# A hybrid diffusion block in fp32 on one Trainium2 core: the weights of one modulation step as one tile and one DMA of 2048 columns

## The chip, the cores and the metric

The kernel runs on one core of a Trainium2 chip. The metric is the device time of one execution in microseconds. Before the change it is 1861.96 us, the median of 3 runs (1861.82 to 1862.53).

## The reference

A backbone block over 512 latent tokens and 256 context tokens of width 1024, with two layers in fp32. Layer 0 mixes with a Hyena long convolution beside a spatial gating unit, layer 1 with a recurrent block (RG-LRU); each layer then has a SwiGLU of inner width 2816. What the change touches is the modulation: each layer scales, shifts and gates by vectors that come from the condition c (latents) and c_ctx (context).

```python
silu_c = jax.nn.silu(c)
silu_cc = jax.nn.silu(c_ctx)
for l in range(DEPTH):
    mod_x = (silu_c @ w_ada[l] + b_ada[l]).reshape(-1, 1, N_MOD, D_MODEL)
    hx = modulate(rmsnorm(x, norm_mix_g[l]), mod_x[:, :, 0], mod_x[:, :, 1])
    ...
        mod_c = (silu_cc @ w_ada[l] + b_ada[l]).reshape(1, 1, N_MOD, D_MODEL)
    ...
    x = x + mod_x[:, :, 2] * mix_x
    hx = modulate(rmsnorm(x, norm_ffn_g[l]), mod_x[:, :, 3], mod_x[:, :, 4])
    x = x + mod_x[:, :, 5] * swiglu(hx, w_ffn_in[l], w_ffn_out[l])
```

w_ada is 2 x 1024 x 6144 in fp32, 50 MB in all: a product of two vectors with a large matrix, which is read once.

## The kernel before, in words

All activations stand with channels on the 128 partitions and tokens along the row. A large product is split in high and low fp32r halves and made of three matmuls (hi by hi, hi by lo, lo by hi). Weights come by DMA from SP's queue into one of three `raw` tiles (`load_w`, L230), are split by `halve` (L247 casts to `whi`, L248 subtracts to `wlo`) on ACT, DVE or POOL, and then stand ready for the PE. SP's queue is in order: a DMA that waits for its tile to come free holds up all that stand behind it.

The modulation is the class `Ada` (L317 to L355). `Ada(l, r)` makes 2048 of the 6144 columns for layer l (r = 0, 1, 2). It has 8 steps, one for each 128 rows of w_ada. In a step k, `load` (L323 to L330) brings 128 x 2048 weights in pieces of `ada["w"]` columns, one tile and one DMA each, from a ring of `ada["b"]` tiles of the pool; `mm` (L332 to L338) makes four matmuls (L336), one for each 512 columns. Each has the 128 x 32 tile `sct` as its stationary operand (columns 0 and 1 hold silu of c and c_ctx for this k, the rest is zero) and writes 32 partitions of one PSUM tile, quarter q to partitions 32q to 32q+31. After step 7 the sums are copied (L341), transposed (L344) and become `mod[l][r]`.

Six of them are made, beside other work: `Ada(0, 0)` and `Ada(0, 1)` in the first 190 us with 3 tiles of 1024 columns, `Ada(0, 2)` in the latent long convolutions (`fwd_x`, `inv_x`, 330 to 392 us) with 4 tiles of 512 columns, and `Ada(1, 0)` to `Ada(1, 2)` in layer 0's SwiGLU (495 to 940 us) with 3 tiles of 512 columns, so that the fourth piece of a step waits for the first piece's matmul. In the SwiGLU `post` calls the steps, one or more after each pair of hidden tiles (the list `fill`). The order on each engine is not the order of the source: the framework's scheduler places every instruction by a simulated timeline when the program is built, and it may put the four matmuls of a step apart with other matmuls between them.

Small constants (gains, biases, convolution taps, c) come as one tile `prm` of 289 columns by one DMA (L212, L213); `pc(name)` returns a slice of it.

Of the kernel before, what the change touches and what calls it, by code (L numbers as in the profile page):

```python
# [8 lines left out]
F32 = mybir.dt.float32  # L9
F32R = mybir.dt.float32r  # L10
I32 = mybir.dt.int32
AF = mybir.ActivationFunctionType
# [4 lines left out]
P = 128  # L17
D = 1024
KD = D // P
# [9 lines left out]
EPS = 1e-6  # L29
# [18 lines left out]
PCOLS = {}  # L48
_n = 0
for _name, _w in (("b_ada0", 48), ("b_ada1", 48), ("mix_g0", 8), ("mix_g1", 8), ("ffn_g0", 8), ("ffn_g1", 8),  # L50
                  ("fin_g", 8), ("hcw", 36), ("hcb", 12), ("skip", 8), ("ln_g", 4), ("rcw", 44), ("rcb", 11),
                  ("lam", 22), ("c", 16)):
    PCOLS[_name] = (_n, _w)
    _n += _w
NPC = _n

PARTS = [[(i, min(i + 4, NPAIR)) for i in range(0, NPAIR, 4)], [(0, 20), (20, 22)]]

# [118 lines left out]
def program(tc, A, out):  # L177
    nc = tc.nc
    act, dve, pool, pe = nc.scalar, nc.vector, nc.gpsimd, nc.tensor
    f = lambda t: t.bitcast(F32)  # L180
# [3 lines left out]
    def op(name, side="left", **kw):  # L184
        cm = tc.tile_pool(name=name, bufs=1, side=side, **kw)
        opened.append(cm)
        return cm, cm.__enter__()

    def cl(cm):
        opened.remove(cm)  # L190
        cm.__exit__(None, None, None)

    _, cst = op("cst")
# [7 lines left out]
    def nm(s):  # L201
        cnt[0] += 1
        return f"{s}_{cnt[0]}"
# [4 lines left out]
    def smt():  # L208
        return ps.tile([P, 512], F32, tag="sm", bufs=4, name=nm("sm"))


    prm = cst.tile([P, NPC], F32, name="prm")  # L212
    nc.sync.dma_start(prm, A["prm"])  # L213

    def pc(name):
        o, w = PCOLS[name]
        return prm[:, o:o + w]

    ident = cst.tile([P, P], F32, name="ident")
    make_identity(nc, ident)  # L220
# [52 lines left out]
    class Job:  # L273
# [6 lines left out]
        def mm(self, b, k):  # L280
            wh, wl = self.w
            xh, xl = self.x(b, k)
            n = self.n[b]
            self.n[b] += 1
            for pi, (w, x) in enumerate(((wh, xh), (wh, xl), (wl, xh))):
                pe.matmul(self.outs[b], w[:, k * P:(k + 1) * P], x,  # L286
                          start=(n == 0 and pi == 0), stop=(n == self.nk - 1 and pi == 2))
# [4 lines left out]
    def newton(pl, src, n, scale, eps, tag):  # L292
        v = pl.tile([P, n], F32, tag=tag + "v", name=nm("nv"))
        y = pl.tile([P, n], F32, tag=tag + "y", name=nm("ny"))
        t = pl.tile([P, n], F32, tag=tag + "t", name=nm("nt"))
        dve.tensor_scalar(v, src, scale, eps, op0=ALU.mult, op1=ALU.add)
        yi = y.bitcast(I32)
        dve.tensor_single_scalar(yi, v.bitcast(I32), 1, op=ALU.logical_shift_right)
        dve.tensor_scalar(yi, yi, -1, 0x5F3759DF, op0=ALU.mult, op1=ALU.add)
        dve.tensor_scalar_mul(v, v, -0.5)  # L300
        for _ in range(3):
            dve.tensor_mul(t, y, v)
            dve.tensor_mul(t, t, y)
            dve.scalar_tensor_tensor(y, t, 1.5, y, op0=ALU.add, op1=ALU.mult)
        return y


    sct = cst.tile([P, KD, 32], F32, name="sct")
    dve.memset(sct, 0.0)
    mod = [[None] * 3, [None] * 3]  # L310
    ada = {"b": 3, "w": 1024}

    class Ada:
# [17 lines left out]
        def mm(self, k):  # L331
            l, r = self.l, self.r  # L332
            if k == 0:
                self.ps = smt()
            for q in range(4):
                pe.matmul(self.ps[32 * q:32 * q + 32, :], sct[:, k, :],  # L336
                          self.w[k, q],
                          start=(k == 0), stop=(k == KD - 1))  # L338
            if k == KD - 1:
                sb = ada["p"].tile([P, 512], F32, tag="ada", bufs=ada["b"], name=nm("adas"))  # L340
                act.copy(sb, self.ps)  # L341
                pt = smt()
                for q in range(4):
                    pe.transpose(pt[:, P * q:P * (q + 1)], sb[:, P * q:P * (q + 1)], ident)  # L344
                m = cst.tile([P, 2, 16], F32, name=f"mod{l}{r}")
                for v in range(2):
                    dve.tensor_add(m[:, v, :].rearrange("p (j q) -> p j q", q=4),
                                   pt.rearrange("p (q j s) -> p j q s", q=4, j=4)[:, :, :, v],
                                   pc(f"b_ada{l}")[:, 16 * r:16 * r + 16].rearrange("p (j q) -> p j q", q=4))
                mod[l][r] = m  # L350
# [9 lines left out]
    def ab(l, which):  # L360
        g = pc(f"mix_g{l}" if which == "mix" else f"ffn_g{l}")
        sc = mod[l][0][:, :, 8:16] if which == "mix" else mod[l][2][:, :, 0:8]
        sh = mod[l][0][:, :, 0:8] if which == "mix" else mod[l][1][:, :, 8:16]
        a = cst.tile([P, 2, 8], F32, name=f"A{l}{which}")
        for v in range(2):
            dve.scalar_tensor_tensor(a[:, v, :], sc[:, v, :], 1.0, g, op0=ALU.add, op1=ALU.mult)
        return a, sh
# [84 lines left out]
    HALF = [(0, 384), (384, 768)]  # L452


    cm_h, hp = op("h")
    cm_ada, ada["p"] = op("ada")
    cm_zb, zb = op("zb", "right")
# [30 lines left out]
    ktl = [kf.tile([P, 1024], F32R, name=f"ktl{i}") for i in range(2)]  # L488
    kdram = {}
    nfil = {}  # L490
    nfs = cst.tile([P, 16], F32, name="nfs")
    for s in "xc":
        for order in range(2):
            nfil[s, order] = 4 * len(nfil)
# [163 lines left out]
    s01.load()  # L658
    ada0.load(1)
    pool.memset(hd2[64:65, :], 1.0)  # L660
    act.activation(sct[:, :, 0], pc("c")[:, 0:8], AF.Silu)
    act.activation(sct[:, :, 1], pc("c")[:, 8:16], AF.Silu)
    s00.prep()
    s10.load_f3w()
    load_x(1)
# [91 lines left out]
    hcw, hcb = pc("hcw"), pc("hcb")  # L757
# [70 lines left out]
    for i, c in enumerate((19, 12, 13, 14, 15)):  # L828
# [6 lines left out]
        for _ in range(2):  # L835
            if len(fill) > 0:
                fill.pop(0)()
    nfy = newton(cst, nfs, 16, 0.5, EPS, "nf")
    cl(cm_nt)
    cl(cm_kf)  # L840
    cm_za, za = op("za", "right")
# [28 lines left out]
    skip = pc("skip")  # L870
# [136 lines left out]
    cl(cm_h)  # L1007
    cm_hy, hy = op("hy")
    ada["p"] = hy
    ada["b"] = 4  # L1010
    ada["w"] = 512
    for i in range(2, 4):
        load_dt(hy, i, dtr[i - 2])
    ada2.load(0)
# [29 lines left out]
    cl(cm_hy)  # L1044
    cl(cm_eo)
    cl(cm_dt)


    _, c2 = op("c2")
    _, xp = op("x")  # L1050
    cm_xc, xc = op("xc")
    cm_ada, ada["p"] = op("adaB")
    ada.update(b=3, w=512)
    cm_nt, ntp = op("ntB")
    cm_g, gp = op("g0")
    xt = []
# [433 lines left out]


    lam = pc("lam")
    sp = [c2.tile([P, 22], F32, name=f"sp{i}") for i in range(5)]
    cq = c2.tile([P, 22], F32, name="cq")
    cq2 = c2.tile([P, 22], F32, name="cq2")
    hba = c2.tile([RDH, 64], F32, name="hba")
# [10 lines left out]
    for cf in (1.0 / 120.0, 1.0 / 24.0, 1.0 / 6.0, 0.5, 1.0, 1.0):  # L1507
        dve.tensor_mul(ee, ee, rr)
        dve.tensor_scalar(ee, ee, cf, None, op0=ALU.add)
    ni = c2.tile([P, 22], I32, name="ni")  # L1510
    dve.tensor_scalar(nn, nn, 127.0, 8388608.0, op0=ALU.add, op1=ALU.mult)
    dve.tensor_copy(ni, nn)
    dve.tensor_mul(ee, ee, ni.bitcast(F32))
# [11 lines left out]
    dve.tensor_scalar_mul(cq, ee, 2.0)  # L1525
    dve.tensor_scalar_mul(cq2, ee, -4.0)
    dve.tensor_scalar_mul(hba, hba, 0.5)
    fill = Ada(1, 0).steps() + Ada(1, 1).steps() + Ada(1, 2).steps()
    cm_hf, hf = op("hf0")

# [15 lines left out]
    rcw, rcb = pc("rcw"), pc("rcb")  # L1546
# [184 lines left out]
    for j in range(NR):  # L1731
        a, b = rg_chunk(j)
# [30 lines left out]
    for b, (t0, t1) in enumerate(BLK1):  # L1763
# [7 lines left out]
        for k in range(KD):  # L1771
            o = hf.tile([P, 256], F32, tag=f"b{k}{'hl'[b]}", name=nm("o"))
# [27 lines left out]
```

## Time and profile before

| | |
|---|---|
| median of 3 runs | 1861.96 us |
| profiled execution: its time | 1861.27 us |
| profiled execution: span from first to last instruction | 1859.5 us |
| mean granted TensorE clock | 0.962 |
| busy: PE, DVE, ACT, POOL | 93%, 68%, 39%, 33% of the span |
| matmuls of the modulation (L336) | 121.1 us of PE busy time, 384 records of 192 matmuls |

A matmul of fp32 operands leaves two records in this profile, so 384 records are 192 matmuls (6 x 8 x 4). The profiled execution's own time is 0.7 us below the median. In a timeline row, columns are start, duration, engine, line, operation, out<-in, shape, count, and in brackets the idle time before it with what ended it. Ends of matmuls are modelled, so what a matmul costs is read from the start before it to the start after it.

### The profile page before, as it was taken

To read this page: it belongs to the slowest core of one execution; us is meant where nothing else is said; L and a number is where in the kernel's file an instruction comes from. 1 tells how busy PE (TensorE), PEld (TensorE's weight loads), DVE (VectorE), ACT (ScalarE), POOL (GpSimd) and SP (SyncE) were. 2 spreads that over 40 slices of the span, in tenths; PEclk is the share of its full clock that TensorE was granted. 3 is DMA by queue.
4 is the path that set the end of the run, shared out by engine and by line. 5 is a ranking of instruction groups with operands and counts; after the bars stand their busy time and mean duration, and the time that the engine had idled before them with its cause. 6 is when DMAs were issued, how large, how long until landed. Compare 5 with 4: busy or idle time off the path is not lost. (4 is left out here: it accounts for less than half of the span.)

```text
span 1859.5 us, 23986 instructions
## 1 busy us (share of the span) xinstructions
PE 1728.6 (93%) x8968; PEld 1433.9 (77%) x8968; DVE 1265.4 (68%) x1963; ACT 726.2 (39%) x1144; POOL 616.6 (33%) x518
## 2 busy tenths in 40 slices
PE   5999999899999999999999988888997799999996
PEld 2576888579868978998798867667786678888886
DVE  7865766566887866887688785879889733333225
ACT  3543333222434333433343435666655332222212
POOL 4332132442465554564545421444444200000002
PEclk8999999899999999999999989889998899999998
DMA  8746232724243343213522124444453132222321
GB/s 285 238 139 229 86 122 81 242 89 142 64 125 112 99 143 123 67 63 119 159 68 69 63 65 129 119 114 116 125 134 93 66 114 91 94 99 80 91 80 46
DMA packets 92077, 213.02 MB, mean 115 GB/s; under 512 B 9001, under 2 KB 34745, under 8 KB 91961
## 3 DMA queue, kind: packets, MB, share of 16 engines
q1 hardware_dynamic: 89593, 204.68, 35.3%
q0 software_dynamic: 1792, 6.29, 0.9%
q8 instruction: 70, 1.15, 0.3%
q10 hardware_dynamic: 576, 0.52, 0.1%
q14 instruction: 46, 0.38, 0.1%
HBM read 178.30 MB, written 11.53 MB: 102 GB/s over the span
## 5 line engine op out<-in xcount | busy, mean ns | idle before, releaser
L248 DVE TENSOR_TENSOR wlo<-raw,whi 128x512 fp32r<-128x512 f32 (+2 forms) x300 | 308.2, 1042 | 275.9 <-ACT whi L247 270.5
L247 ACT CAST whi<-raw 128x1024 fp32r<-128x1024 f32 (+2 forms) x228 | 193.7, 858 | 415.4 <-PE mm L263 178.5
L386 POOL TENSOR_TENSOR ssum<-ssum,sq 128x256 f32<-128x256 f32 (+2 forms) x37 | 37.7, 1022 | 443.7 <-ACT sq L384 423.2
L336 PE MATMUL sm<-ada,sct 128*32 128x512 f32 x384 | 121.1, 635 | 3.9 <-issue 3.0
L1104 PE MATMUL sm<-yh,whi 128*128 128x256 f32 (+1 forms) x304 | 96.4, 323 | 21.8 <-DVE x L1067 11.1
L248 POOL TENSOR_TENSOR wlo<-raw,whi 128x1024 fp32r<-128x1024 f32 (+1 forms) x31 | 76.4, 2464 | 111.8 <-DVE whi L247 38.8
L286 PE MATMUL sm<-hh,whi 128*128 128x512 f32 (+1 forms) x248 | 93.5, 378 | 7.2 <-ACT whi L247 4.0
L1104 PE MATMUL sm<-yh,wlo 128*128 128x256 f32 (+1 forms) x304 | 95.9, 317 | 1.8 <-POOL wlo L248 1.8
L286 PE MATMUL sm<-hh,wlo 128*128 128x256 f32 (+1 forms) x248 | 92.4, 378 | 5.0 <-DVE wlo L248 2.9
L1104 PE MATMUL sm<-yl,whi 128*128 128x256 f32 (+1 forms) x304 | 95.9, 316 | 0.0
L286 PE MATMUL sm<-hl,whi 128*128 128x512 f32 (+1 forms) x248 | 92.3, 372 | 0.0
L247 DVE CAST whi<-raw 128x512 fp32r<-128x512 f32 (+2 forms) x103 | 67.9, 660 | 33.8 <-PE sm L1279 26.1
L1104 PEld LDWEIGHTS sm<-yh,whi 128*128 128x128 f32 x304 | 60.8, 202 | 25.8 <-DVE x L1067 12.2
L263 PE MATMUL mm<-hl,whi 128*128 128x512 f32 (+1 forms) x256 | 69.2, 344 | 0.0
L263 PE MATMUL mm<-hh,wlo 128*128 128x512 f32 (+1 forms) x256 | 68.9, 346 | 0.0
L263 PE MATMUL mm<-hh,whi 128*128 128x512 f32 (+1 forms) x256 | 67.8, 344 | 0.0
L1643 ACT ACTIVATE tg<-mm,hba 88x768 f32<-88x768 f32 x64 | 55.3, 891 | 25.9 <-PE mm L263 14.9
L1104 PEld LDWEIGHTS sm<-yh,wlo 128*128 128x128 f32 x304 | 61.1, 201 | 2.0 <-POOL wlo L248 2.0
L286 PEld LDWEIGHTS sm<-hh,whi 128*128 128x128 f32 x248 | 49.4, 199 | 16.8 <-ACT whi L247 5.6
L1321 POOL TENSOR_TENSOR u<-u,u 128x384 f32<-128x384 f32 x40 | 51.2, 1280 | 31.5 <-ACT u L1320 31.5
L1104 PEld LDWEIGHTS sm<-yl,whi 128*128 128x128 f32 x304 | 61.3, 202 | 0.2
L286 PEld LDWEIGHTS sm<-hh,wlo 128*128 128x128 f32 x248 | 49.5, 201 | 15.1 <-DVE wlo L248 5.0
(943 smaller groups left out, 5303.3 us busy)
## 6 DMA issues: line engine op xcount, KB each, us to landing
raw<-in_wfi_dram SPq DMA_DIRECT2D x88, 512.0 KB
ada<-in_w_ada_dram SPq DMA_DIRECT2D x144, 256.0 KB
raw<-in_wfo_dram SPq DMA_DIRECT2D x38, 512.0 KB
ada<-in_w_ada_dram SPq DMA_DIRECT2D x24, 512.0 KB
raw<-in_wio_dram SPq DMA_DIRECT2D x22, 512.0 KB
raw<-in_wie_dram SPq DMA_DIRECT2D x20, 512.0 KB
th<-tg SPq DMA_DIRECT2D x12, 528.0 KB
kk<-kdx SPq DMA_DIRECT2D x16, 384.0 KB
```

The costliest lines, as they stand in the source:

```text
L247: (h_.tensor_copy if h_ is not act else act.copy)(hi, src)
L248: l_.tensor_sub(lo, src, f(hi))
L263: pe.matmul(o, w, xx, start=(k == 0 and pi == 0), stop=(k == n - 1 and pi == 2))
L286: pe.matmul(self.outs[b], w[:, k * P:(k + 1) * P], x, start=(n == 0 and pi == 0), stop=(n == self.nk - 1 and pi == 2))
L336: pe.matmul(self.ps[32 * q:32 * q + 32, :], sct[:, k, :], self.w[k, q], start=(k == 0), stop=(k == KD - 1))
L386: (dve if late else pool).tensor_add(self.s[b], self.s[b], q)
L1104: pe.matmul(pa, w[:, c], x[k][:, t0 - off:t1 - off], start=(i == 0 and pi == 0), stop=(i == n - 1 and pi == 2))
L1321: pool.tensor_add(v, v, u)
L1643: act.activation(h3(t[:, mi, :]), m[0:RDH, :, 0:384], AF.Tanh, bias=hba[:, b:b + 1], scale=0.5)
```

## The change

In the long convolutions and in layer 0's SwiGLU each step of `Ada` gets one tile of 2048 columns and one DMA of 1024 KB, with one such tile in the ring, in place of four tiles and four DMAs of 256 KB (rings of 4 and 3 tiles). A tile of 2048 columns is 2 KB a partition more than 3 of 512, so room is made: `sct` shrinks from 256 to 46 columns (a step's stationary operand is now a window of 32 columns that starts at column 2k, so columns 2 to 31 hold other values; the rows of PSUM that they feed are not read), constants that are used only up to the long convolutions move with `nfs` to a pool `p0` that is closed there, which makes two DMAs of the one for `prm`, and scratch of the recurrent block's constants moves to a pool `sp` that is closed before the SwiGLU.

```diff
-                  ("fin_g", 8), ("hcw", 36), ("hcb", 12), ("skip", 8), ("ln_g", 4), ("rcw", 44), ("rcb", 11),
-                  ("lam", 22), ("c", 16)):
+                  ("fin_g", 8), ("rcw", 44), ("rcb", 11), ("lam", 22),
+                  ("c", 16), ("hcw", 36), ("hcb", 12), ("skip", 8), ("ln_g", 4)):
...
+NPL = PCOLS["c"][0]
...
-    prm = cst.tile([P, NPC], F32, name="prm")
-    nc.sync.dma_start(prm, A["prm"])
+    prm = cst.tile([P, NPL], F32, name="prm")
...
-        return prm[:, o:o + w]
+        return prm[:, o:o + w] if o < NPL else prm0[:, o - NPL:o - NPL + w]
...
-    sct = cst.tile([P, KD, 32], F32, name="sct")
-    dve.memset(sct, 0.0)
+    sct = cst.tile([P, 2 * KD + 30], F32, name="sct")
+    dve.memset(sct[:, 2 * KD:], 0.0)
...
-                pe.matmul(self.ps[32 * q:32 * q + 32, :], sct[:, k, :],
-                          self.w[k, q],
+                pe.matmul(self.ps[32 * q:32 * q + 32, :], sct[:, 2 * k:2 * k + 32], self.w[k, q],
                           start=(k == 0), stop=(k == KD - 1))
...
+    cm_p0, p0 = op("p0")
+    prm0 = p0.tile([P, NPC - NPL], F32, name="prm0")
+    nc.sync.dma_start(prm0, A["prm"][:, NPL:NPC])
+    nc.sync.dma_start(prm, A["prm"][:, 0:NPL])
...
     ada["p"] = hy
-    ada["b"] = 4
-    ada["w"] = 512
+    ada["b"] = 1
+    ada["w"] = 2048
...
     cl(cm_dt)
+    cl(cm_p0)
...
     cm_ada, ada["p"] = op("adaB")
-    ada.update(b=3, w=512)
+    ada.update(b=1, w=2048)
...
-    sp = [c2.tile([P, 22], F32, name=f"sp{i}") for i in range(5)]
+    cm_sp, spp = op("sp")
+    sp = [spp.tile([P, 22], F32, name=f"sp{i}") for i in range(5)]
```

The scheduler makes a new order from this. Three places show it (an entry's `x4` is four equal instructions in a row; the line of the matmul is L336 before and L338 after).

PE in layer 0's SwiGLU, where the first steps of `Ada(1, 0)` are multiplied between the matmuls of the first jobs (L286, L287; `whi` and `wlo` are halves of weights, 384 columns each). Before, the last piece of step 0 (`ada_4834`) and the first of step 1:

```order
L286 MATMUL sm_4472<-q0h_4464,wlo_4488 128x384
L336 MATMUL sm_4836<-ada_4834,sct 32x512
L286 MATMUL mm_4469<-c1h_4450,whi_4475 128x384
L286 MATMUL mm_4470<-c1h_4450,whi_4481 128x384
L286 MATMUL sm_4472<-c1h_4450,whi_4487 128x384
L336 MATMUL sm_4836<-ada_4841,sct 32x512
L286 MATMUL mm_4469<-c1l_4451,whi_4475 128x384
L286 MATMUL mm_4469<-c1h_4450,wlo_4476 128x384
L286 MATMUL mm_4470<-c1l_4451,whi_4481 128x384
L286 MATMUL mm_4470<-c1h_4450,wlo_4482 128x384
L286 MATMUL sm_4472<-c1l_4451,whi_4487 128x384
L286 MATMUL sm_4472<-c1h_4450,wlo_4488 128x384
```

After the change, at the second step of the same `Ada`:

```order
L287 MATMUL mm_4431<-q0h_4426,whi_4437 128x384
L287 MATMUL mm_4432<-q0h_4426,whi_4443 128x384
L287 MATMUL sm_4434<-q0h_4426,whi_4449 128x384
L338 MATMUL sm_4792<-ada_4797,sct 32x512 x4
L287 MATMUL mm_4431<-q0l_4427,whi_4437 128x384
L287 MATMUL mm_4431<-q0h_4426,wlo_4438 128x384
L287 MATMUL mm_4432<-q0l_4427,whi_4443 128x384
L287 MATMUL mm_4432<-q0h_4426,wlo_4444 128x384
```

Single matmuls of a step that stood apart now stand as four in a row. Over the three `Ada` of the SwiGLU, runs of such matmuls fall from 64 (22, 21, 21) to 35 (9, 13, 13).

PE in the latent long convolutions, second step of `Ada(0, 2)`, between the transforms (L263, L264; `Y` the spectra, `dth` and `dtl` the transform matrix, 256 columns each). Before, two of its pieces:

```order
L263 MATMUL sm_3182<-eo_3086,dth_2695 128x256 x2
L263 MATMUL sm_3182<-eo_3086,dtl_2696 128x256
L336 MATMUL sm_3073<-ada_3080,sct 32x512
L263 MATMUL sm_3098<-dth_2965,Y_3047 128x256
L263 MATMUL sm_3098<-dtl_2966,Y_3047 128x256
L263 MATMUL sm_3130<-dth_2965,Y_3047 128x256
L263 MATMUL sm_3130<-dtl_2966,Y_3047 128x256
L336 MATMUL sm_3073<-ada_3082,sct 32x512
L263 MATMUL sm_3098<-dth_2965,Y_3047 128x256
```

After the change:

```order
L264 MATMUL sm_3123<-dtl_2971,Y_3046 128x256
L264 MATMUL sm_3091<-dth_2970,Y_3046 128x256
L264 MATMUL sm_3123<-dth_2970,Y_3046 128x256
L338 MATMUL sm_3072<-ada_3077,sct 32x512 x4
L264 MATMUL sm_3091<-dth_2970,Y_3069 128x256
L264 MATMUL sm_3091<-dtl_2971,Y_3069 128x256
L264 MATMUL sm_3123<-dth_2970,Y_3069 128x256
L264 MATMUL sm_3123<-dtl_2971,Y_3069 128x256
```

Here 23 runs become 10. In the first 190 us, where the tiles are as before, the scheduler makes 23 runs of what were 21.

SP's queue in the SwiGLU, the loads of `Ada(1, 0)` (`ada`) among those of the SwiGLU's weights (`raw`). Before:

```order
L327 DMA ada_4945<-in_w_ada_dram 128x512
L327 DMA ada_4947<-in_w_ada_dram 128x512
L230 DMA raw_5076<-in_wfi_dram 128x1024
L327 DMA ada_4949<-in_w_ada_dram 128x512
L327 DMA ada_4951<-in_w_ada_dram 128x512
L327 DMA ada_5145<-in_w_ada_dram 128x512
L230 DMA raw_5078<-in_wfi_dram 128x1024
L327 DMA ada_5147<-in_w_ada_dram 128x512
L327 DMA ada_5149<-in_w_ada_dram 128x512
L327 DMA ada_5151<-in_w_ada_dram 128x512
L1414 DMA raw_5241<-in_wfo_dram 128x2x512
L327 DMA ada_5157<-in_w_ada_dram 128x512
```

After the change:

```order
L329 DMA ada_4797<-in_w_ada_dram 128x2048
L329 DMA ada_4883<-in_w_ada_dram 128x2048
L329 DMA ada_4889<-in_w_ada_dram 128x2048
L231 DMA raw_5014<-in_wfi_dram 128x1024
L329 DMA ada_5083<-in_w_ada_dram 128x2048
L231 DMA raw_5016<-in_wfi_dram 128x1024
L1420 DMA raw_5167<-in_wfo_dram 128x2x512
L329 DMA ada_5089<-in_w_ada_dram 128x2048
L1420 DMA raw_5271<-in_wfo_dram 128x2x512
L329 DMA ada_5222<-in_w_ada_dram 128x2048
L1420 DMA raw_5347<-in_wfo_dram 128x2x512
L329 DMA ada_5695<-in_w_ada_dram 128x2048
```

Where four loads stood for a step there is one; of the loads of weights none, one or two stand between the loads of two steps here. Each load of a step now waits for all four matmuls of the step before, since there is one tile.

From PE's 5375th entry on (5288th after the change) the scheduler's order differs in the recurrent block of layer 1 too, though no source line of it changed.

## Rows read from the trace of the kernel before

**Rows 1.** The page: span, and busy time of each engine with its count.

```profile
span 1859.5 us, 23986 instructions
PE 1728.6 (93%) x8968; PEld 1433.9 (77%) x8968; DVE 1265.4 (68%) x1963; ACT 726.2 (39%) x1144; POOL 616.6 (33%) x518
```

**Rows 2.** Windows: stretch, length, busy time of each engine (count), clock, DMA share, GB/s.

```profile
330.00:340.00 10.00, 7.77 (x24) 3.65 (x25) 8.65 (x12) 2.47 (x4) 6.69 (x6) 0.50 1.03 371
330.00:392.00 62.00, 59.17 (x304) 34.41 (x305) 39.62 (x52) 12.01 (x19) 31.55 (x27) 0.92 0.66 218
500.00:550.00 50.00, 47.39 (x223) 32.91 (x218) 46.70 (x55) 23.59 (x43) 34.17 (x26) 1.00 0.39 123
635.00:740.00 105.00, 104.78 (x525) 81.88 (x524) 74.44 (x108) 36.82 (x71) 51.35 (x45) 1.00 0.41 128
740.00:844.00 104.00, 100.56 (x560) 97.74 (x559) 87.99 (x131) 41.42 (x80) 56.76 (x47) 0.98 0.23 74
1100.00:1465.00 365.00, 308.56 (x1649) 262.93 (x1647) 304.95 (x372) 212.18 (x256) 141.76 (x85) 0.91 0.42 116
```

**Rows 3.** Timeline of PE, layer 0's SwiGLU: a run of one and one of three matmuls.

```profile
562.00 0.33 PE L1279 MATMUL sm<-t1h,wlo 128*128 128x384 f32 x1
562.18 0.34 PE L1279 MATMUL sm<-t2h,whi 128*128 128x384 f32 x1
562.44 1.05 PE L336 MATMUL sm<-ada,sct 128*32 128x512 f32 x2
563.42 0.45 PE L1279 MATMUL sm<-t2l,whi 128*128 128x384 f32 x1
...
570.93 1.06 PE L336 MATMUL sm<-ada,sct 128*32 128x512 f32 x6
571.92 0.45 PE L1279 MATMUL mm<-q0h,whi 128*128 128x384 f32 x1
```

**Rows 4.** Timeline of PE, first 190 us: a run of four matmuls from two tiles.

```profile
158.18 1.06 PE L336 MATMUL sm<-ada,sct 128*32 128x512 f32 x8
159.17 0.50 PE L263 MATMUL mm<-hh,whi 128*128 128x512 f32 x1
```

**Rows 5.** Timeline of PE, long convolutions: a run of one.

```profile
380.45 0.28 PE L263 MATMUL sm<-dth,Y 128*128 128x256 f32 x1
380.66 1.04 PE L336 MATMUL sm<-ada,sct 128*32 128x512 f32 x2
381.64 0.39 PE L263 MATMUL sm<-dth,Y 128*128 128x256 f32 x1
```

**Rows 6.** Waits of SP's queue: who waited for whom, us in total, times, longest.

```profile
SPq L327 <- PE sm L336: 251.2, 90, 17.9
```

**Rows 7.** Chain of waits, recurrent block (start, us, what): transfers of up to 528 KB.

```profile
1309.58 2.69 DMA th<-tg
...
1390.09 6.22 DMA th<-tg
```

**Rows 8.** Timeline of PE: gaps in the SwiGLU and the long convolutions.

```profile
330.48 1.93 PE L336 MATMUL sm<-ada,sct 128*32 128x512 f32 x8 [3.02 <-issue]
...
536.89 0.45 PE L1279 MATMUL mm<-t3h,whi 128*128 128x384 f32 x1 [1.35 <-ACT t3h L255]
...
785.37 0.44 PE L1279 MATMUL sm<-q1h,whi 128*128 128x384 f32 x1 [1.16 <-ACT q1h L255]
786.57 0.45 PE L1279 MATMUL sm<-p0ah,whi 128*128 128x384 f32 x1 [0.76 <-DVE whi L247]
```

**Rows 9.** Windows after two of those gaps (columns as in rows 2).

```profile
537.00:540.50 3.50, 3.50 (x12) 1.46 (x12) 3.50 (x6) 3.22 (x7) 1.38 (x1) 1.00 0.46 146
787.00:790.50 3.50, 3.50 (x14) 3.50 (x13) 3.50 (x6) 0.51 (x1) 2.02 (x3) 0.53 0.02 5
```

**Rows 10.** Timeline at the start: SP's first issue, PE's first matmul.

```profile
0.75 0.39 SPq L213 DMA_DIRECT2D prm<-in_prm_dram  x1
...
5.18 2.82 PE L474 MATMUL sm<-mlp 33*64 33x384 f32 x4 [5.18 <-DMA mlp<-in_mlp_dram]
```

More of the change, by code (lines that the diff above doesn't have):

```diff
@@ L490, in program @@
     nfil = {}
-    nfs = cst.tile([P, 16], F32, name="nfs")
+    nfs = p0.tile([P, 16], F32, name="nfs")
     for s in "xc":
@@ L660, in program @@
     pool.memset(hd2[64:65, :], 1.0)
-    act.activation(sct[:, :, 0], pc("c")[:, 0:8], AF.Silu)
-    act.activation(sct[:, :, 1], pc("c")[:, 8:16], AF.Silu)
+    for v in range(2):
+        act.activation(sct[:, 0:2 * KD].rearrange("p (k v) -> p v k", v=2)[:, v], pc("c")[:, 8 * v:8 * v + 8], AF.Silu)
     s00.prep()
@@ L837, in program @@
                 fill.pop(0)()
-    nfy = newton(cst, nfs, 16, 0.5, EPS, "nf")
+    nfy = newton(p0, nfs, 16, 0.5, EPS, "nf")
     cl(cm_nt)
@@ L1509, in program @@
         dve.tensor_scalar(ee, ee, cf, None, op0=ALU.add)
-    ni = c2.tile([P, 22], I32, name="ni")
+    ni = spp.tile([P, 22], I32, name="ni")
     dve.tensor_scalar(nn, nn, 127.0, 8388608.0, op0=ALU.add, op1=ALU.mult)
@@ L1527, in program @@
     dve.tensor_scalar_mul(hba, hba, 0.5)
+    cl(cm_sp)
     fill = Ada(1, 0).steps() + Ada(1, 1).steps() + Ada(1, 2).steps()
```

## The prediction

> **What bounds the kernel.** I began with the page: PE is busy for 93% of the span, DVE for 68% [rows 1]. An average hides stages, so the windows came next. In the stretch of layer 0's SwiGLU with the second of its three modulation products PE is busy for 104.78 of 105 us and DVE for 71%; in the stretch behind it, with no modulation, PE has 3.44 us idle in 104 and DVE is at 85% [rows 2]. So PE sets the pace there, and time that leaves PE's queue shortens the kernel until DVE, which makes the weights, comes up to it. At the head of the SwiGLU it nearly has: between 500 and 550 us DVE is busy for 46.70 of 50 [rows 2]. In the long convolutions PE is busy for 59.17 of 62 us, with the first ten at half clock [rows 2].
>
> The row to look at is what a modulation matmul costs PE. A matmul of the SwiGLU starts 0.18 us after the one before (562.00, 562.18). With one modulation matmul between, it is 562.18 to 563.42: 1.24 us, less 0.17 for the first one's own turn, so the run costs 1.07 us [rows 3]. A run of three takes from 570.93 to 571.92, 0.99 us, and a run of one from 562.44 to 563.42, 0.98 [rows 3]. A run of four, from two tiles in the first 190 us, takes 0.99 [rows 4]. The four quarters of a step write different partitions, and in a row they run together: **PE pays for a run, not for a matmul**. In the long convolutions a run costs 1.19 less 0.12 (two thirds of 0.17), again 1.07 us [rows 5].
>
> **The change, part by part.**
>
> Runs: the changed order has 29 fewer in the SwiGLU (64 to 35) and 13 fewer in the long convolutions (23 to 10). At 1.07 us each that is 31.0 and 13.9 us off PE, 44.9 in all.
>
> New wait: with one tile, the load of a step is issued when the step before has been multiplied, and lands while PE does what the order puts between. No trace shows a load of 1024 KB, so I bound it. A transfer of 528 KB takes 2.69 us from issue to landing on the chain, in a crowd 6.22 [rows 7]. The core moved 371 GB/s with all DMA engines busy [rows 2], so 496 KB more take 1.4 us: 4.1 us alone, 5.5 with one load of 512 KB ahead, 7.6 if every load is as late as that slow transfer (3.5 us later). I take 5.5, since a load or two of weights or spectra stands between most steps in SP's new order.
>
> Against it I count the matmuls between a step and the next in PE's new order. In the SwiGLU they are 36, 33, 52, 44, 50, 48, 35 for the first modulation product and 70, 48, 33, 27, 42, 42, 48 for each of the two others; at 0.174 us that is 6.3, 5.7, 9.0, 7.7, 8.7, 8.4, 6.1 and 12.2, 8.4, 5.7, 4.7, 7.3, 7.3, 8.4 us. Only the two gaps of 4.7 fall short of 5.5: 1.6 us of stall (none at 4.1, 15.5 at 7.6). In the long convolutions the gaps are 3.5, 6.3, 3.0, 4.9, 5.0, 2.2, 6.3 us: 8.9 us of stall at 5.5 (3.6 at 4.1, 22.0 at 7.6).
>
> The Trainium skill (DMA: Bandwidth & Descriptors, section "Measured" under Bandwidth) lists 6.15 us for moving 1 MB by the software path; no run here shows such a load, and 528 KB in 2.69 us speaks for less. By 6.15 us the stalls would be 4 and 12 us, and the time 6 us more than my sum.
>
> Clock: after the 3.02 us gap at 330.48 the granted clock is at half (1.2 GHz) for the ten microseconds to 340, and after 1.16 and 0.76 us in short order for 3.5 us; a gap of 1.35 us alone left it full [rows 2, 8, 9]. A fall costs about half of 3.5 us, so 1.6. Of the stalls in the long convolutions three are of 2.0 to 3.3 us; I let two lower the clock: 3.2 us (0 to 5).
>
> DVE as the next bound: at the head of the SwiGLU some 8 of the runs go, but DVE leaves 3.3 us in that stretch [rows 2], so 5 us of the gain are lost. In the second and third products DVE's share goes from 71% to 77%, not quite half of the way to the 85% at which PE idles for 3.3%: 1.5 us each. Together 8 us (0 to 16).
>
> SP: 96 issues fewer. SP's queue waits for the modulation's matmuls for 251.2 us, in 90 waits [rows 6]; it will go on waiting there, in fewer and longer waits, while the loads of weights behind it have three tiles in hand. I cost it at nothing; if those tiles run dry, it shows as PE waiting for `whi` or `wlo`, and that is within the 16 above.
>
> The start: one DMA issue more ahead of `mlp`, whose landing releases PE's first matmul at 5.18 us; an issue takes 0.39 us [rows 10], so 0.5 us. Two runs more in the first 190 us at up to 1.07 us, some of it in time that PE has idle: 1.5 us. Zeroing a smaller `sct`, and the pools that open and close, lie beside other work or wait for tiles that were read long before: nothing.
>
> The recurrent block: its order changed with no edit. PE idles there for 56.4 of 365 us [rows 2], waiting for others. I take 0, and as bounds two transfers that come 3.5 us later, or earlier [rows 7]: 7 us either way.
>
> **The sum**: 44.9 less 1.6, 8.9, 3.2, 8 and 2 is 21.2 us. The profiled execution took 1861.3 us, which gives 1840.1; the median of the runs is 0.7 us above it, so **1841 us**.
>
> **The rivals.**
>
> *The loads come in time and nothing else binds*: landing at 4.1 us, no DVE term, no fall of the clock. Then 44.9 less 3.6 and 2, so 1823 us. For it: PE's 104.78 of 105 us. Against it: DVE's 46.70 of 50. Chance 0.16.
>
> *DVE takes over all through the SwiGLU*, so that only 40% of 31.0 us (3.3 of 8) comes through, 12.4 in place of 21.4: 1850 us. For it: PE already waits for weights where no modulation runs. Against it: DVE's 71%. Chance 0.14.
>
> *The single tile becomes the wait* (slower): every load lands after 7.6 us, as the 6.22 us transfer did, since it waits for its tile and then stands behind weights. PE stalls for 37.5 us, ten of the stalls are of 1.9 us or more and each costs 1.6 us of clock, 16; with 2 for the start that is 55.5 against 44.9: 1872 us. It decides from a landing of about 7.2 us on. For it: gaps of 2.2 to 5.7 us in ten places. Against it: the 2.69 us row. Chance 0.07. The rule behind it stands in the Trainium skill (Trainium Kernel Development and Optimization, section Best Practices): "Double-buffer for performance: Overlap DMA with compute". The change does the reverse; the trace before shows no ring of one.
>
> *No change*: the recurrent block's 7 us and the costs above at their upper ends eat the gain: about 1861. Chance 0.05.
>
> *The change does not do what it says*: four in a row from one tile run one after the other. Then 128 matmuls cost 0.98 us each where 87 runs did: 40 us more, 1902. Rows 4 speak against it, though their four come from two tiles. Chance 0.02.
>
> **The numbers.** My own case has 0.56, and its own range is 1831 to 1850 (the recurrent block's 7 us and half of the DVE term). The range is 1822 to 1856: it adds the first two rivals and leaves the others out. Under 0.2% (3.7 us) cannot be told from no change here. Faster is 0.56 + 0.16 + 0.14 = 0.86, the same 0.05, slower 0.07 + 0.02 = 0.09.
>
> **What would show it.** Right: runs of eight records (four matmuls) at 1.0 us; the busy time of the modulation's matmuls down by about 40 us; 32 loads of 1024 KB; short waits of PE for `ada` between 330 and 390 us; DVE's share up in the SwiGLU, and that stage some 21 us shorter. Wrong: PE waiting for `ada` in the SwiGLU for more than 10 us in all, half-clock stretches there, or a recurrent block that moves by more than 7 us.

## The result, and the profile after

The changed kernel takes 1836.15 us (median of 4 runs, 1832.47 to 1839.97) against 1862.24 us before (4 runs, 1861.82 to 1863.28): ratio 0.9861, 95% interval 0.9848 to 0.9873. The forecast was 1841, its range 1822 to 1856. The profiled execution took 1839.97 us, 1838.2 of them span; a second profile, taken later, has 1835.22 us.

The profiled one is the slowest of the four. The page after: the span, the busy times, the group of modulation matmuls and the issues of their loads:

```profile
span 1838.2 us, 23815 instructions
PE 1695.2 (92%) x8968; PEld 1436.0 (78%) x8968; DVE 1271.3 (69%) x1963; ACT 726.6 (40%) x1144; POOL 622.0 (34%) x518
L338 PE MATMUL sm<-ada,sct 128*32 128x512 f32 x384 | 77.6, 630 | 4.7 <-DMA ada<-in_w_ada_dram 3.0
...
ada<-in_w_ada_dram SPq DMA_DIRECT2D x32, 1024.0 KB
```

The group of modulation matmuls on the page before:

```profile
L336 PE MATMUL sm<-ada,sct 128*32 128x512 f32 x384 | 121.1, 635 | 3.9 <-issue 3.0
```

PE is busy for 33.4 us less with as many matmuls (8968) [rows 1], and the 384 records of the modulation's matmuls went from 121.1 us to 77.6.

A run of four from one tile, PE's timeline at the head of the SwiGLU (start, us, engine, line, what):

```profile
492.89 0.34 PE L287 MATMUL sm<-q0h,whi 128*128 128x384 f32 x1
493.15 1.06 PE L338 MATMUL sm<-ada,sct 128*32 128x512 f32 x8
494.15 0.44 PE L287 MATMUL mm<-q0l,whi 128*128 128x384 f32 x1
```

From the matmul ahead to the one behind it is 1.26 us, as 1.24 for a run of one [rows 3]: four matmuls cost PE what one did.

To see where the time came from, I cut both traces at the same places in the program: the first modulation matmul of the long convolutions; the first matmul behind them (`sm<-yh,whi`); the first `mm<-q0h,whi` of the SwiGLU; its end (the next `sm<-ones,ssum`); the first `mm<-xh,whi` of the recurrent block; the first `b0h` matmul of layer 1's SwiGLU. The three stretches that matter are the long convolutions, the SwiGLU and what I call the block behind. The windows of the kernel before (columns as in [rows 2]):

```profile
330.48:404.86 74.38, 68.76 (x383) 43.80 (x383) 48.92 (x68) 16.44 (x25) 36.02 (x30) 0.94 0.56 184
498.79:1070.32 571.53, 558.53 (x2922) 479.67 (x2923) 448.17 (x646) 221.20 (x422) 301.78 (x256) 0.99 0.32 101
1121.29:1478.78 357.49, 299.58 (x1631) 257.72 (x1630) 299.18 (x383) 209.66 (x255) 136.17 (x83) 0.90 0.41 115
```

The same of the changed kernel, and a stretch at the head of its SwiGLU:

```profile
331.65:398.36 66.71, 54.74 (x384) 42.65 (x385) 51.73 (x92) 16.55 (x25) 38.15 (x31) 0.94 0.59 209
492.44:1042.99 550.55, 531.10 (x2922) 478.85 (x2923) 456.03 (x646) 221.10 (x422) 305.35 (x256) 0.99 0.31 104
1093.65:1457.57 363.92, 303.80 (x1632) 261.64 (x1630) 300.49 (x383) 210.58 (x255) 134.66 (x83) 0.89 0.40 113
513.80:520.60 6.80, 5.54 (x16) 5.07 (x17) 6.80 (x8) 2.35 (x4) 3.68 (x4) 0.50 0.20 78
```

The start is 1.2 us longer (330.48 to 331.65), the long convolutions 7.7 shorter, the SwiGLU 21.0 shorter, and the block behind 6.4 **longer**; the rest differs by 0.2. In the SwiGLU PE's busy time fell by 27.4 us, of which the clock hid some: by the records of the granted clock it stood at half (1.2 GHz) for 6.8 us of this stage before and for 13.8 after, and such a stretch costs half its length, so 3.5 us more. 27.4 and 3.5 are 30.9 us; 29 runs at 1.07 us are 31.0. In the long convolutions PE's busy time fell by 14.0 us; half clock there went from 9.6 us to 7.5, which is 1.0 of the 14.0, so 13.0 are left where 13 runs are 13.9. **The price per run held**; what it bought is less by what PE then idles or runs at half clock.

### The profile page after: what moved, and what is told of

Same layout as the page of the kernel before. It is cut to its first block, busy times and chain, and to the rows that moved or that the text cites. A ratio compares the mean times of both kernels' runs of the same rounds, so it can differ in the third digit from the quotient of the medians.

```text
span 1838.2 us, 23815 instructions
## 1 busy us (share of the span) xinstructions
PE 1695.2 (92%) x8968; PEld 1436.0 (78%) x8968; DVE 1271.3 (69%) x1963; ACT 726.6 (40%) x1144; POOL 622.0 (34%) x518
## 5 line engine op out<-in xcount | busy, mean ns | idle before, releaser
L1110 PE MATMUL sm<-yh,whi 128*128 128x256 f32 (+1 forms) x304 | 97.5, 327 | 21.3 <-DVE x L1073 12.9
L287 PE MATMUL sm<-hh,whi 128*128 128x512 f32 (+1 forms) x248 | 94.9, 383 | 10.3 <-ACT whi L248 5.7
L287 PE MATMUL sm<-hh,wlo 128*128 128x256 f32 (+1 forms) x248 | 92.8, 380 | 3.5 <-POOL wlo L249 2.8
L287 PE MATMUL sm<-hl,whi 128*128 128x512 f32 (+1 forms) x248 | 93.5, 377 | 0.0
L338 PE MATMUL sm<-ada,sct 128*32 128x512 f32 x384 | 77.6, 630 | 4.7 <-DMA ada<-in_w_ada_dram 3.0
L264 PE MATMUL mm<-hl,whi 128*128 128x512 f32 (+1 forms) x256 | 69.4, 346 | 0.0
L264 PE MATMUL mm<-hh,wlo 128*128 128x512 f32 (+1 forms) x256 | 69.1, 347 | 0.0
L264 PE MATMUL mm<-hh,whi 128*128 128x512 f32 (+1 forms) x256 | 68.1, 345 | 0.0
L287 PEld LDWEIGHTS sm<-hh,whi 128*128 128x128 f32 x248 | 50.5, 203 | 21.0 <-ACT whi L248 8.1
L287 PEld LDWEIGHTS sm<-hh,wlo 128*128 128x128 f32 x248 | 50.4, 204 | 12.6 <-POOL wlo L249 3.2
```

The source lines that it names most:

```text
L264: pe.matmul(o, w, xx, start=(k == 0 and pi == 0), stop=(k == n - 1 and pi == 2))
L287: pe.matmul(self.outs[b], w[:, k * P:(k + 1) * P], x, start=(n == 0 and pi == 0), stop=(n == self.nk - 1 and pi == 2))
L338: pe.matmul(self.ps[32 * q:32 * q + 32, :], sct[:, 2 * k:2 * k + 32], self.w[k, q], start=(k == 0), stop=(k == KD - 1))
L1110: pe.matmul(pa, w[:, c], x[k][:, t0 - off:t1 - off], start=(i == 0 and pi == 0), stop=(i == n - 1 and pi == 2))
```

## The experiments

Theory **T**: PE pays 1.07 us for each run of modulation matmuls, and only what PE doesn't then wait for comes through. Rival **R1**: the 96 DMA issues fewer on SP are the gain. **R2**: the room and the other addresses are. **O**, added when the first runs were in: the block behind is longer where its order on PE is another.

All runs in one table. Runs of modulation matmuls, lengths of the three stretches and PE's busy time in the SwiGLU are from the profile of each; "half" is its time at half clock in the SwiGLU. The medians of the kernel before beside them were 1862.2 to 1863.0.

| kernel | median us | ratio, 95% | runs: long conv., SwiGLU | long conv. us | SwiGLU us (PE busy; half) | block behind us |
|---|---|---|---|---|---|---|
| before | 1862.24 | | 23, 64 | 74.4 | 571.5 (558.5; 6.8) | 357.5 |
| changed | 1836.15 | 0.9848 to 0.9873 | 10, 35 | 66.7 | 550.6 (531.1; 13.8) | 363.9 |
| e1 ring of four | 1866.74 | 1.0012 to 1.0031 | 23, 58 | 76.3 | 570.6 (555.7; 6.8) | 360.2 |
| e2 four DMAs, columns | 1864.15 | 1.0000 to 1.0023 | 22, 52 | 79.2 | 565.1 (549.5; 10.2) | 360.0 |
| e3 four DMAs, rows | 1867.62 | 1.0014 to 1.0037 | 10, 37 | 75.8 | 571.3 (537.1; 27.3) | 364.9 |
| e4 all runs of four | 1833.26 | 0.9823 to 0.9856 | 8, 24 | 71.9 | 542.6 (519.6; 13.7) | 357.7 |
| e5 four in SwiGLU | 1827.59 | 0.9788 to 0.9817 | 10, 24 | 68.7 | 542.7 (520.8; 17.1) | 357.5 |
| e6 SwiGLU alone | 1841.65 | 0.9864 to 0.9893 | 23, 35 | 75.7 | 549.2 (529.7; 13.7) | 357.6 |
| e7 long conv. alone | 1856.97 | 0.9954 to 0.9979 | 10, 64 | 66.8 | 572.1 (558.7; 3.4) | 360.1 |
| e8 two tiles of 1024 | 1850.18 | 0.9911 to 0.9941 | 15, 52 | 72.0 | 560.2 (543.7; 0) | 359.9 |
| e9 third place too | 1839.84 | 0.9865 to 0.9912 | 10, 24 | 71.4 | 542.3 (520.4; 13.7) | 357.8 |
| e10 six steps left out | 1823.63 (one run) | | 10, 6 | 66.4 | 542.0 (509.0; 27.3) | 357.6 |
| e11 changed, again | 1835.22 (one run) | | 10, 35 | 66.4 | 548.9 (529.3; 10.2) | 363.5 |

**e1, a ring of four in the same room.** Against the changed kernel:

```diff
-    ada["b"] = 1
-    ada["w"] = 2048
+    ada["b"] = 4
+    ada["w"] = 512
...
-    ada.update(b=1, w=2048)
+    ada.update(b=4, w=512)
```

> The changed kernel's room, parameters and start, but modulation weights again in a ring of four tiles of 512 columns, four DMAs a step, in the SwiGLU and in the long convolutions. Runs of modulation matmuls on PE in its order: 23 in the long convolutions and 58 in the SwiGLU (before 23 and 64, changed kernel 10 and 35). Theory T (PE pays for each run): the changed kernel got 21.0 us for 29 runs in the SwiGLU and 7.7 us for 13 in the long convolutions, 0.72 and 0.59 us a run with its stalls; so 6 runs fewer than before give 4.3 us, the start takes 1.2: 1859 us, up to 1865 if the stages behind the SwiGLU again give back the 6 us that they did in the changed kernel. Rival R1 (the gain is the 96 DMA issues saved on SP): about 1862, no lower. Rival R2 (the gain is the room and the other addresses): about 1836.

Measured 1866.74 us, 4.3 more than before. R2 falls: room, addresses and start bring no gain, they cost (in this profile 2.6 us at the start, 2.0 in the long convolutions, 2.7 in the block behind). T's range is missed too, by 2; the 6 runs fewer gave 1.0 us in the SwiGLU. By T's price PE's busy time there should fall by 6.4 us and fell by 2.8, at an equal half-clock time: the modulation's own matmuls took 6.0 less (67.1 to 61.1 us), the others 2.4 more, for a cause that no run shows.

**e2, one tile, four DMAs by columns.**

```diff
-                nc.sync.dma_start(w, A["w_ada"][self.l, P * k:P * (k + 1), c0:c0 + n])
+                for p in range(0, n, min(n, 512) if n == 2048 else n):
+                    e = p + (512 if n == 2048 else n)
+                    nc.sync.dma_start(w[:, p:e], A["w_ada"][self.l, P * k:P * (k + 1), c0 + p:c0 + e])
```

> One tile of 2048 columns as in the changed kernel, but filled by four DMAs of 512 columns, so that each quarter's matmul may start when its own quarter has landed. The order then has 22 runs in the long convolutions and 52 in the SwiGLU. T: 12 runs more than the changed kernel at 0.59 us and 17 more at 0.72 us, 19 us more: about 1855 (1848 to 1862). R1 (DMA issues): as before the change, 1862. R2 (room): 1836.

1864.15 us, T's range missed by 2; R1's 1862 is nearer than T's 1855. The wide tile alone gives nothing in all: the four loads let the scheduler set the quarters apart, 22 and 52 runs. PE's busy time in the SwiGLU fell by 9.1 us and 1.7 more went to the clock: 10.8 for 12 runs, 12.8 by T's price. But the long convolutions are 4.9 us longer than before, and the block behind 2.5.

**e3, one tile, four DMAs by rows.**

```diff
-                nc.sync.dma_start(w, A["w_ada"][self.l, P * k:P * (k + 1), c0:c0 + n])
+                for p in range(0, P, 32 if n == 2048 else P):
+                    e = p + (32 if n == 2048 else P)
+                    nc.sync.dma_start(w[p:e], A["w_ada"][self.l, P * k + p:P * k + e, c0:c0 + n])
```

> The same tile and the same number of DMAs as the run above, but each brings 32 rows of all 2048 columns, so that all four quarters become ready together: the order has 10 runs in the long convolutions and 37 in the SwiGLU, two more than the changed kernel. T: the time of the changed kernel within 5 us, 1833 to 1842. R1 (DMA issues): 1862, since it issues as many DMAs as the kernel before. R2: 1836, as T; the run above tells these two apart.

1867.62 us, 26 above T's range, and the time looks like R1's. The page's group of modulation matmuls tells them apart:

```profile
L340 PE MATMUL sm<-ada,sct 128*32 128x512 f32 x384 | 82.0, 654 | 31.6 <-DMA ada<-in_w_ada_dram 26.9
```

PE's time for the matmuls fell, to 82.0 us, with as many DMA issues as before: PE's saving doesn't hang on their number. By whole times alone R1 isn't out, as none of e1 to e3, with the issues of before, is faster than before; in the SwiGLU of e5 below, with the changed kernel's issues and 11 runs fewer, 7.9 us more come off. But PE waits 26.9 us for the tile, 13 times, and after such gaps it is at half clock. Busy time down by 21.4 us, and 10.3 (a half of 20.5 us more at half clock), make 31.7 us in the SwiGLU, and 27 runs are 28.9; every bit of it is given back. This is the rival "the single tile becomes the wait", made by a load that lands later. The traces also record when a load raises its semaphore for the last time, and so when a whole step has landed (no view shown here lists it). From the first issue of a step that is, in the median of 32 steps, 4.9 us with one DMA (changed kernel), 5.8 with four by columns (e2) and 7.1 with four by rows. The last of the four is issued 1.3 us after the first in both. So e2 has 0.9 us of lateness with the same four issues, and the 32 rows go with 1.3 more.

**e4, runs of four alone.** The scheduler is told to set a step's matmuls ahead of other ready work:

```diff
-            for q in range(4):
-                pe.matmul(...)
+            with tc.high_priority(offset=600 if ada["w"] == 2048 else 0):
+                for q in range(4):
+                    pe.matmul(...)
```

> The changed kernel with the four matmuls of a step set ahead of other ready work, so that the order has runs of four alone: 8 in the long convolutions and 24 in the SwiGLU, 13 fewer than the changed kernel. T: at 0.72 and 0.59 us a run 9 us less, about 1827; at the full 1.07 us 14 us less, 1822. A rival, that DVE already sets the pace of the SwiGLU: 1833 to 1839, no change. R1 and R2: 1836. If the earlier matmuls stall PE for their load: more PE waits for the modulation tile than the changed kernel has, and up to 5 us slower.

1833.26 us, 6 us above T's first figure and at the lower end of the rival's range; the whole time doesn't decide. By stages it is clearer. Windows of its long convolutions and its SwiGLU:

```profile
331.19:403.05 71.86, 55.79 (x384) 43.94 (x385) 54.10 (x95) 17.28 (x26) 38.62 (x30) 0.87 0.56 196
496.64:1039.27 542.63, 519.58 (x2922) 477.44 (x2923) 457.25 (x646) 219.69 (x422) 302.94 (x256) 0.99 0.32 106
```

The SwiGLU lost 28.9 us for 40 runs (busy time 39.0 less, half clock 3.4: 42.4; 40 at 1.07 are 42.8). The long convolutions, with two runs fewer than the changed kernel, are 5.2 us longer: PE waits there for 16.1 us, 4.25 of them in one wait for the tile, and the granted clock is 0.87.

**e5, runs of four in the SwiGLU alone**: the edit of e4 with `offset=600 if self.l else 0`.

> The changed kernel with the four matmuls of a step set ahead of other ready work in the SwiGLU alone; the long convolutions keep the changed kernel's order. Runs: 10 and 24. Behind the SwiGLU PE's order is again that of the kernel before, but for a dozen rows. T (each run costs PE 1.07 us, and what PE then waits or runs at half clock is given back): long convolutions 7.7 us shorter than before as in the changed kernel, SwiGLU 29 us shorter as in the run with all runs of four, start 1 us later, recurrent block 0 to 2 us shorter: about 1826, range 1820 to 1831. Theory O (the recurrent block is 6 to 8 us longer where its order on PE is the one that the changed kernel has) gives the same; its rival, that the recurrent block is longer whenever modulation is faster, gives 1833. If runs behind a load that is late cost more than they save: 1836 or more.

1827.59 us against 1826 expected, and the fastest kernel here that computes everything: 0.9803 of before, where the changed kernel has 0.9861. It keeps e4's SwiGLU, and the block behind is at 357.5 us. Its SwiGLU:

```profile
495.07:1037.76 542.69, 520.84 (x2922) 479.49 (x2923) 458.69 (x646) 219.68 (x422) 303.81 (x256) 0.98 0.31 106
```

Its long convolutions gain 5.7 us and not the 7.7 expected: with the changed kernel's order on PE, half clock takes 14.0 us of them where it takes 7.5 in that kernel.

**e6 and e7, one place each.** e6 keeps `ada["b"] = 4`, `ada["w"] = 512` in the long convolutions; e7 has `ada.update(b=3, w=512)` in the SwiGLU.

> One tile of 2048 columns in the SwiGLU alone (35 runs); the long convolutions keep four tiles of 512 (23 runs). PE's order behind the SwiGLU is that of the kernel before, but for a dozen rows. T with O: SwiGLU 21 us shorter than before, long convolutions and start 4 us longer as with the ring of four in the same room, recurrent block 0 to 2 us shorter: about 1844, range 1838 to 1848. Without O (recurrent block 6 us longer as in the changed kernel): 1851.

> One tile of 2048 columns in the long convolutions alone (10 runs); the SwiGLU has three tiles of 512 as before the change (64 runs). PE's order behind the SwiGLU is that of the kernel before. T: long convolutions 7.7 us shorter, start 1 us later, the rest as before or up to 4 us longer: about 1857, range 1853 to 1860. R2 (the room alone brings the gain): 1836.

1841.65 and 1856.97 us, both where T (and, for e6, O) put them. e6 has the changed kernel's 35 runs and its SwiGLU within 1.4 us, but the block behind as before. Its window:

```profile
1100.56:1458.19 357.63, 297.83 (x1631) 256.46 (x1630) 298.56 (x383) 209.59 (x255) 134.36 (x83) 0.91 0.41 115
```

The last column of the table falls into groups by PE's order behind the SwiGLU, which no edit touches. Where it is that of the kernel before or differs in 12 rows of 3432 (before, e4, e5, e6, e9, e10), the block takes 357.5 to 357.8 us; with 2 to 8 other rows, further on (e1, e2, e7, e8), 359.9 to 360.2; with the changed kernel's order, about a thousand rows of it changed (changed, e3, e11), 363.5 to 364.9. In that order DVE, ACT, POOL and SP have other orders there too, so which engine's order costs the 6 us isn't shown.

**e8, two tiles of 1024**: `ada["b"] = 2`, `ada["w"] = 1024`, and `ada.update(b=2, w=1024)`.

> Two tiles of 1024 columns in place of one of 2048, two DMAs a step, so that half a step loads while the other half is multiplied: the double buffering that the changed kernel gives up. Runs: 15 in the long convolutions and 52 in the SwiGLU. T: 8 and 12 runs fewer than before, 8.6 and 12.8 us off PE, of which half to two thirds come through as in the changed kernel; start 1 us later: about 1851, range 1845 to 1858. Rival B (a load that is in time matters more than the number of runs): 1836 or less, with PE's waits for the modulation tile below 1 us in all.

1850.18 us against 1851. Two tiles give the overlap back and still lose to one: half-steps arrive apart, which makes 52 runs in the SwiGLU. Nor did PE stop waiting: 7.4 us for modulation tiles in all (5.0 in the long convolutions, 2.4 in the SwiGLU), where the changed kernel has 3.0. So B's condition, waits below 1 us, was never met, and B isn't tested.

**e9, the wide tile in the third place too.** In the kernel of e5:

```diff
-    ada = {"b": 3, "w": 1024}
+    ada = {"b": 1, "w": 2048}
...
-            with tc.high_priority(offset=600 if self.l else 0):
+            with tc.high_priority(offset=600 if self.l or self.r == 1 else 0):
...
+    w19 = ada["p"].tile([P, 2048], F32R, tag="ada", bufs=ada["b"], name=nm("w19"))
...
-                    *[ada["p"].tile([P, 1024], F32R, tag="ada", bufs=ada["b"], name=nm("w19")) for _ in range(2)])
+                    *[w19[:, 1024 * v:1024 * v + 1024] for v in range(2)])
```

> The kernel with runs of four alone in the SwiGLU, and the one tile of 2048 columns also for layer 0's second modulation product, which runs between 130 and 190 us: 8 runs of four there in place of 11. In that stretch PE is busy for 60.0 of 60 us. T: 3 runs at 1.07 us, 3 us less than that kernel's 1827.6 if no load is late: about 1824.5, range 1822 to 1828. Rival (the one tile becomes the wait where DMA moves 208 GB/s already): PE waits for the modulation tile before 190 us, and 1829 or more.

1839.84 us, 12 slower than e5, as the rival had it. SP's waits between 100 and 215 us and PE's between 20 and 195 in e9 (who for whom, us, times, longest):

```profile
SPq L329 <- DMA ada<-in_w_ada_dram: 18.4, 5, 7.1
...
PE sm L339 <- DMA ada<-in_w_ada_dram: 4.9, 1, 4.9
```

In e5 the first of these is 2.4 us. PE's wait of 4.9 us isn't in the second product: it ends at 76.61 us, in the first, four of whose steps the edit gives the one wide tile too. In the second product a step follows the one before in 7.8 to 10.2 us, since the one tile must be multiplied and then filled again; the last load is issued at 195.28 us, in e5 at 177.27. SP's order puts other loads behind it, and PE's products of the last filters behind the modulation. The timelines of SP and PE in e9:

```profile
195.28 0.33 SPq L329 DMA_DIRECT2D ada<-in_w_ada_dram  x1
...
215.33 0.33 SPq L852 DMA_DIRECT2D sgw<-in_sw_dram  x1
...
207.48 0.81 PE L619 MATMUL sm<-pf,ktc 128*128 128x256 f32 x3
```

and in e5:

```profile
177.27 0.33 SPq L329 DMA_DIRECT2D ada<-in_w_ada_dram  x1
...
199.21 0.33 SPq L851 DMA_DIRECT2D sgw<-in_sw_dram  x1
...
189.87 0.60 PE L619 MATMUL sm<-pf,ktc 128*128 128x256 f32 x2
```

16 to 18 us late; PE then has a gap of 5.34 us at 216.97, and the long convolutions start 12.3 us later than in e5. Up to there PE idles for 33.9 us (26.0 in e5), these 4.9 and 5.3 among them, and is busy 4.4 us longer. The Trainium skill (Trainium Kernel Development and Optimization, section Best Practices) says "Double-buffer for performance: Overlap DMA with compute". The first 190 us agree with it. The SwiGLU doesn't: there SP issues the changed kernel's loads of a product 6.1 to 20.1 us apart (the first of all, far ahead, aside), 20 of the 24 land within 6 us, PE waits 0.5 us for them, and the kernel with one wide tile beats the one with two of half the size.

**e10, six of eight steps left out.**

```diff
             for q in range(4):
+                if l and 0 < k < KD - 1:
+                    continue
```

> The changed kernel without the matmuls of the middle six of the eight steps of each modulation product in the SwiGLU (their loads stay): 6 runs there in place of 35. It tells what the SwiGLU is bound by when modulation is nearly gone; PE's order behind it is that of the kernel before. If PE alone sets the pace, 58 runs fewer than before take 62 us off the SwiGLU's 571.5: 509.5 us, and the kernel at about 1792. If the share that came through so far (28.8 of 42.8 us) holds: 42 us, SwiGLU about 530, kernel 1813. If DVE takes over (it is busy for 82 of 100 us already): SwiGLU 535 or more, kernel 1818 or more, DVE's share at 85% or above.

One execution, 1823.63 us. The SwiGLU takes 542.0 us, 0.7 less than with 24 runs (e4, e5), where two profiles of the changed kernel are 1.6 apart: of the last 18 runs nothing that can be told comes through. What PE saves there goes to idle time and to half clock, 27.3 us of it. Windows of e10, the whole SwiGLU and 100 us of it:

```profile
491.22:1033.18 541.96, 508.95 (x2779) 480.31 (x2779) 463.22 (x646) 219.69 (x422) 312.40 (x256) 0.97 0.31 106
...
600.00:700.00 100.00, 95.56 (x524) 89.23 (x523) 84.72 (x120) 39.03 (x76) 56.24 (x47) 0.97 0.42 148
```

PE idles for 33.0 us in the SwiGLU (13.0 before). For whom, between 500 and 1025 us:

```profile
PE sm L1287 <- ACT s L1301: 7.4, 15, 1.6
PE sm L1287 <- DVE wlo L249: 5.5, 14, 0.7
PE sm L1287 <- ACT q1h L256: 4.9, 4, 1.4
PE mm L1287 <- ACT u L1305: 2.8, 1, 2.8
PE sm L1287 <- DVE whi L248: 2.8, 4, 0.9
```

It came out as the third case said, but the next bound is not DVE's weights alone: 15.1 us of these waits end on ACT and 8.3 on DVE, which is busy for 85 of 100 us.

**e11, the changed kernel again.**

> The changed kernel itself, for a second profile. Theory O (the longer recurrent block belongs to its order on PE): the block from its first to its last input matmul again 290 to 293 us, where the seven kernels with the other order have 283 to 285. If it was chance: 283 to 285. Long convolutions: 66.7 us again if what they lose is set by the order, up to 69 if half-clock stretches fall by chance.

From the first to the last input matmul of the recurrent block 290.7 us (291.4 in the first profile; 285.1 before; 283.2 to 283.7 in the nine others), and the long convolutions 66.4: O holds, as far as it says that the longer block comes with that order. The long convolutions hold at 66.4 to 66.8 in four profiles with that order on PE (changed, e7, e10, e11), but e5 and e9 have the same order there and 68.7 and 71.4 us, with half clock for 14.0 and 17.1 us in place of 7.5: half-clock stretches do move them. The 4.8 us between the two spans lie in the SwiGLU (1.6), behind it up to the recurrent block (1.5), at the start (0.8), and in smaller pieces.

## Why the prediction was right, and where it wasn't

**Runs, 44.9 us: right.** Busy time and half clock account for 30.9 of 31.0 us in the SwiGLU and 13.0 of 13.9 in the long convolutions. The other kernels bear the price out for many runs: 42.4 us for 40 (e4), 59.8 for 58 (e10). For few it is blurred: 10.8 us for 12 (e2), and 2.8 for 6 (e1), where 6.4 were due.

**SwiGLU, 21.4 us net: measured 21.0, and 22.6 in the second profile.** Stalls on the tile were 0.5 us (forecast 1.6). The term called DVE, 8 us, was right in size: PE's idle time rose by 6.5 us and the clock took 3.5. Its place was right too: at the head PE waits 2.78 and 1.55 us for `whi` at 511.68 and 514.19, and the granted clock is then at half (the window of 6.8 us above). Half-clock stretches in the SwiGLU were one of my signs of being wrong; this one came, and took 3.4 us. The cause was right for the most part. PE's waits in the SwiGLU for `whi` from DVE, before and after:

```profile
PE sm L1279 <- DVE whi L247: 1.5, 2, 0.8
...
PE sm L1285 <- DVE whi L248: 5.8, 4, 2.8
```

With fewer runs still, ACT comes in too (e10). Of the rivals, "nothing binds" falls (PE idles 19.5 us there), and "DVE takes over", with 12.4 us, put the point too early: from 35 runs to 24 the SwiGLU still gained 8 us (e4, e5), from 24 to 6 no more than 0.7 (e10).

**Long convolutions, 1.8 us net: measured 7.7. This step failed.** The stalls, 8.9 us in my sum, came to 2.5 us (0.6 before); the clock, 3.2 in my sum, took nothing, as half clock went from 9.6 us to 7.5; and a wait that I had priced at nothing came instead. By the windows PE's busy time fell by 14.02 us and its idle time rose by 6.35, 4.1 of it for the spectra. Waits of PE in the long convolutions, first before, then after the change:

```profile
PE sm L263 <- DVE Y L932: 1.0, 1, 1.0
PE sm L336 <- DMA ada<-in_w_ada_dram: 0.6, 1, 0.6
...
PE sm L263 <- ACT Y L931: 0.3, 1, 0.3
```

```profile
PE sm L264 <- POOL Y L937: 2.9, 2, 1.6
PE sm L338 <- DMA ada<-in_w_ada_dram: 2.5, 2, 1.6
...
PE sm L264 <- DVE Y L937: 1.3, 1, 1.3
PE sm L264 <- ACT Y L936: 1.2, 1, 1.2
```

For the spectra (`Y`) that is 5.4 us, where the kernel before has 1.3.

The landing that I took, 5.5 us, was good. By the semaphores the changed kernel's 32 loads of 1024 KB land 4.7 to 8.8 us after their issue, 5.5 in the mean and 4.9 in the median. The slowest in the long convolutions, SP's issue and PE's matmul that waited for it, 7.3 us apart:

```profile
354.12 0.33 SPq L329 DMA_DIRECT2D ada<-in_w_ada_dram  x1
...
361.40 1.06 PE L338 MATMUL sm<-ada,sct 128*32 128x512 f32 x8 [1.56 <-DMA ada<-in_w_ada_dram]
```

The Trainium skill (DMA: Bandwidth & Descriptors, section "Measured" under Bandwidth) lists 6.15 us for moving 1 MB by the software path. The median of these loads, 4.9 us, is below it, and the 6 us more that I drew from it didn't come.

What failed is the time between two steps, which I had taken as the matmuls in it at two thirds of 0.174 us each. From a load's issue to the matmul that needs it, less PE's wait for it, the seven times are 9.9, 6.5, 5.7, 5.1, 5.2, 4.7 and 6.8 us, where I had 3.5, 6.3, 3.0, 4.9, 5.0, 2.2 and 6.3. The three short ones, which carried most of the 8.9 us, are the ones in which PE waits for the spectra: 2.5, 1.6 and 1.4 us, and 6.4 us of the first are at half clock. The load lands meanwhile, so these waits stand in place of the stalls and not on top of them.

**Recurrent block, 0 within 7 us: 6.4 us lost,** in the range, but I had no ground for the 0. The loss comes with the order that the scheduler chose there; how that order costs it isn't shown.

**Start, 2 us:** 1.2 in the first profile and 0.4 in the second. **SP, 0:** its waits for the modulation's matmuls went from 251.2 us in 90 [rows 6] to 162.9 in 45.

So 1841 for 1836 was in part luck: it rests on two errors that offset each other, 6 us too little from the long convolutions and 6 too little lost behind; the first profile is 21.3 us below that of before, the sum said 21.2, and the second profile and the medians 26. "The single tile becomes the wait" didn't happen, but its mechanism is real: e3 shows it with 26.9 us of PE's waits and e9 with 18.4 of SP's. "The change doesn't do what it says" fell with the first run of eight records.

## What to carry to other kernels

Count what an engine pays for: here a run of up to four matmuls to different partitions, whatever their number. Then a load's form is worth as much as its size, since it decides whether the four become ready together: one DMA of the whole step cut the runs in the SwiGLU from 64 to 35, four by columns into the same tile to 52, and four by rows to 37, but these landed too late to gain by it. After that, read the order of the stretches that nobody edited: a scheduler's other choice went with a loss of 6.4 of 27.7 us, and one priority on the four matmuls brought the old order there back.

## What the hardware showed that I had not expected

Four DMAs of 32 rows that bring the same 1024 KB into the same tile left PE waiting 26.9 us where one DMA left it 3.0. The four landed 7.1 us after the first issue in the median, four by columns 5.8 us, the one 4.9 us. A load of 256 KB was ready 2.85 us after its issue at one of the places in e2 where PE waited (timelines of SP and PE):

```profile
358.43 0.81 SPq L331 DMA_DIRECT2D ada<-in_w_ada_dram  x2
...
361.28 2.62 PE L340 MATMUL sm<-ada,sct 128*32 128x512 f32 x6 [0.82 <-DMA ada<-in_w_ada_dram]
```

In the kernel before, such loads from 320 us on land after 3.2 us in the median (115 of 128, whose landing is on record in full), so four times the bytes in one DMA took 1.6 times as long. And PE's clock takes its share of every gain: of the 29 runs' 31 us in the SwiGLU, 6.5 became idle time and 3.5 went to 7 us more at half clock behind those gaps.
